# Moving the split weights of a hybrid decoder layer to four different offsets in SBUF

## The chip, the cores and the metric

The kernel runs on one core of a Trainium2 chip. The metric is the device time of one execution in microseconds (us). Before the change it is 892.13 us, the median of three runs (890.99 to 892.81).

## The reference

One decoder layer on x of 512 tokens by 1024 features, in float32: a feed-forward block, a mixing block, and a second feed-forward block, each added to x.

```python
x = x + 0.5 * swiglu(rms_norm(x, g_ffn1), w_ffn1_gate, w_ffn1_up, w_ffn1_down)   # hidden width 2816
h = rms_norm(x, g_mix)
q, k, v, u, mq = split(h @ w_in)          # 512, 128, 128, 512, 256 columns
a = sliding_window_attention(rope(norm(q)), rope(norm(k)), v, sinks)     # 8 heads, window 128
b = conformer_conv(u)                     # GLU, depthwise conv of 31 taps, layer norm, swish
c = memory_cross_attention(norm(mq), mk, mv)   # 4 heads over 256 memory tokens
x = x + concat([a, b, c]) @ w_out
x = x + 0.5 * swiglu(rms_norm(x, g_ffn2), w_ffn2_gate, w_ffn2_up, w_ffn2_down)
```

where `swiglu(h, g, u, d) = (silu(h @ g) * (h @ u)) @ d`.

## The kernel before

**Products in three matmuls.** Features lie in SBUF with the feature index on the 128 partitions and tokens along the free axis. To keep float32 accuracy with one-pass matmuls (type fp32r), each operand is split into a rounded part and the rest, hi and lo, and a product is the sum of three matmuls: hi weights by hi features, hi weights by lo features, lo weights by hi features. `mm3` (L330 to L332) does this for 512 tokens at once, the function `product` (L434 to L436) for 256 tokens. Weights are the operand that is loaded into the array (PEld in the profile), features the one that is moved through it. While one matmul runs, the weights of the next are loaded, so at any time TensorE reads two places of SBUF: the moving tile, and the next weight tile.

**Weights.** The class `Weights` holds a list of loads and of items to be split, in the order in which they are used. `load_to` brings 128x1024 float32 tiles from memory on SyncE's queue (tag `wraw`, four buffers). `split_to` makes hi on ScalarE (L158) and lo on VectorE (L159), three items ahead of use. The hi tiles take turns over four buffers, the lo tiles over four others. In the feed-forward blocks four of the 22 hidden tiles are done directly (gate and up products over eight feature tiles). The other 18 use a fast scheme with seven products of 256 columns instead of eight: `make_sums` adds parts of gate and up weights on VectorE, and the features come as combinations made in `blocks` (tiles `bh` and `bl`). Of the seven products' weights six come from the ring and the seventh from a half tile (`vhi`, `vlo`, 512 columns) with one buffer of its own. Between the fast products stand the down-projections, groups of 512-column matmuls on `hh` and `hl`.

**Mixing.** The order of its steps is written out by hand in the list `ORDER`: projections on 512 columns (`xh`, `xl`), convolution taps on VectorE, scores, softmax, transposes, value products, output products (`yh`, `yl`). `ln_mean` takes the mean over the convolution's channels as a matmul with a constant tile `avg` of 1/256, which `consts` fills on GpSimd at the beginning of the mixing block.

**Where tiles lie.** Each pool is laid out in one piece, a tag after another in the order of their first use, with every tile rounded up to 32 bytes per partition. The ring of weights begins at a multiple of 256: four raw tiles, four hi and four lo tiles of 4096 bytes each, so all of them are at 0 mod 256, and so is the end of this pool. The pool of temporaries begins with a filler of 128 bytes; after it and the small tiles, the pool `act`, which holds the split features (`xh`, `xl`, `hh`, `hl` and part of `yh`, `yl`), begins at 64 mod 256. The pools of the two feed-forward blocks and of mixing follow after it in the same place, one at a time. `ffn` puts a filler of `shift` bytes first (0 in the first block, 64 in the second), and a filler of 192 minus `shift` after the block features. So `bh` and `bl` lie at 64 mod 256 in the first block and at 128 in the second, and the half weight tiles at 0 in both. The distance from a weight tile up to the moving tile, mod 256, is therefore 64 everywhere except for the second block's features, where it is 128. In the memory projection (L630 to L632) the roles are exchanged: weights are moved and features loaded.

Of the kernel before, what the change touches and what calls it, by code (L numbers as in the profile page):

```python
# [28 lines left out]
F32 = mybir.dt.float32  # L29
F32R = mybir.dt.float32r  # L30
# [6 lines left out]
P = 128  # L37
# [10 lines left out]
C_G1, C_GM, C_G2, C_GMEM = 0, 8, 16, 24  # L48
# [26 lines left out]
N_ACT = 20  # L75

SUM_BUFS = 3
MEM_F = 17
B_T3, B_Q1, B_Q2, B_T4, B_21, B_22, B_11 = range(7)


class Weights:
# [5 lines left out]
    def __init__(self, nc, pool, dma_ahead, conv_ahead, bufs):  # L88
        self.nc, self.pool = nc, pool
        self.dma_ahead, self.conv_ahead, self.bufs = dma_ahead, conv_ahead, bufs  # L90
        self.loads, self.items = [], []
        self.raw, self.after, self.split, self.piece = {}, {}, {}, {}
        self.sums = {}
        self.extra = None
        self.by_hand = 2
        self.loaded = self.done = self.at = 0

    def add(self, ap):

# [16 lines left out]
    def make_sums(self, i):  # L116
        nc = self.nc
        g, u = self.raw[i], self.raw[i + 1]
        s12 = self.extra.tile([P, 1024], F32, tag="sum", name=f"s12_{i}", bufs=SUM_BUFS)
        s43 = self.extra.tile([P, 1024], F32, tag="sum", name=f"s43_{i}", bufs=SUM_BUFS)  # L120
        l, r = slice(0, 512), slice(512, 1024)
# [6 lines left out]
    def load_to(self, n):  # L128
        while self.loaded < min(n, len(self.loads)):
            i = self.loaded  # L130
            ap = self.loads[i]
            raw = self.pool.tile([P, 1024], F32, tag="wraw", name=f"wraw{i}", bufs=self.bufs[0])
            self.raw[i] = raw
            if i >= self.by_hand:
                to = raw[:, : int(np.prod(ap.shape[1:]))]
                if len(ap.shape) == 3:
                    to = to.rearrange("p (a b) -> p a b", a=ap.shape[1])
                self.nc.sync.dma_start(to, ap)
            self.loaded += 1

    def split_to(self, n):
        nc = self.nc
        while self.done < min(n, len(self.items)):
            i = self.done
            need, cols, tag, src = self.items[i]
            self.load_to(need + 1)
            if need in self.after:
                self.after.pop(need)()
            pool = self.pool if tag == "w" else self.extra
            width = 1024 if tag == "w" else 512  # L150
            bufs = self.bufs[1:] if tag == "w" else (1, 1)
            hi = pool.tile([P, width], F32R, tag=tag + "hi", name=f"{tag}hi{i}", bufs=bufs[0])
            lo = pool.tile([P, width], F32R, tag=tag + "lo", name=f"{tag}lo{i}", bufs=bufs[1])
            if i < self.by_hand:
                self.piece[i] = (src(), hi, lo)
            else:
                raw = src()
                nc.scalar.copy(hi[:, :cols], raw[:, :cols])  # L158
                nc.vector.tensor_tensor(lo[:, :cols], raw[:, :cols], hi[:, :cols].bitcast(F32), op=ALU.subtract)  # L159
            self.split[i] = (hi, lo)  # L160
            self.done += 1
            if i >= self.by_hand:
                self.load_to(need + 1 + self.dma_ahead)
# [33 lines left out]
def layer(tc, ctx, a):  # L197
    nc = tc.nc
    PE, ACT, DVE, POOL = nc.tensor, nc.scalar, nc.vector, nc.gpsimd

    keep = ctx.enter_context(tc.tile_pool(name="keep", bufs=1))
    wpool = ctx.enter_context(tc.tile_pool(name="wpool", bufs=1))
    tmp = ctx.enter_context(tc.tile_pool(name="tmp", bufs=1))
# [4 lines left out]
    def nm(s):  # L208
        uid[0] += 1
        return f"{s}_{uid[0]}"  # L210
# [14 lines left out]
        return tmp.tile([P, n], F32, tag=f"s{n}", name=nm("s"), bufs=6)  # L225


    W = Weights(nc, wpool, dma_ahead=3, conv_ahead=3, bufs=(4, 4, 4))

    def flat(w):  # L230
        return w.rearrange("p k m -> p (k m)")

    def ffn_weights(n, memory):
        gu = a[f"wgu{n}"]

        def down(r, g):
            lo, hi = ROUNDS[r]
            m = per_load(r)
            return a[f"wd{n}"][g * m : (g + 1) * m, :, lo:hi].rearrange("d p k m -> p d (k m)")

        for f in range(NF):
            pre, mid, post = steps(f)
            for d in pre:
                W.add(down(*d))
            if f < N_DIRECT:
                W.add(flat(gu[f, 0]))
                W.add(flat(gu[f, 1]))
            else:
                W.add_pair(flat(gu[f, 0]), flat(gu[f, 1]), [down(*d) for d in mid])
            for d in post:  # L250
                W.add(down(*d))
            if memory and f == MEM_F:
                for t in range(2):
                    W.add(flat(a["wmk"][t]))
                for c in range(2):
# [17 lines left out]
    par = keep.tile([P, C_N], F32, name="par")  # L273
    ident = keep.tile([P, P], F32, name="ident")
    x = keep.tile([P, KT, T], F32, name="x")
    tmp.tile([P, 32], F32, name="shift")
    act = ctx.enter_context(tc.tile_pool(name="act", bufs=1))
    xh, xl = {}, {}

# [102 lines left out]
    def ffn(pool, norm, first, gain, hooks, next_gain, last, shift):  # L382
# [24 lines left out]
        def blocks(k):  # L407

            raw = pool.tile([P, 4, 256], F32, tag="sum", name=nm("braw"), bufs=SUM_BUFS)
            made = pool.tile([P, 4, 256], F32, tag="sum", name=nm("bmade"), bufs=SUM_BUFS)  # L410
            flat_raw = raw.rearrange("p a b -> p (a b)")
# [136 lines left out]
    norm = Norm()  # L548
# [156 lines left out]
    hooks = {9: [rotary]}  # L705
    hooks[MEM_F - 3] = [lambda: load(0), lambda: load(1)]
    hooks[MEM_F - 2] = [lambda: piece(0), lambda: piece(1), lambda: load(2), lambda: load(3)]
    hooks[MEM_F - 1] = [lambda: piece(2), lambda: piece(3)]
    hooks[MEM_F], hooks[MEM_F + 1] = [sums, p1], [p2]
    with tc.tile_pool(name="fast1", bufs=1) as pool:  # L710
        norm = ffn(pool, norm, STARTS, C_G1, hooks, C_GM, False, 0)

    with tc.tile_pool(name="mix", bufs=1) as mix:
        norm = mixing(tc, nc, a, mix, W, norm, locals())

    with tc.tile_pool(name="fast2", bufs=1) as pool:
        ffn(pool, norm, [[0, 1, 2, 3, 4, 5, 6], [7]], C_G2, {}, None, True, 64)


def mixing(tc, nc, a, mix, W, norm, e):  # L720
    PE, ACT, DVE, POOL = nc.tensor, nc.scalar, nc.vector, nc.gpsimd
    mm_bank, sc_bank, tp_bank, work, small = (e[n] for n in ("mm_bank", "sc_bank", "tp_bank", "work", "small"))
# [12 lines left out]
    vtok = mix.tile([P, NB, P], F32, name="vtok")  # L735
    for i in range(2):
        POOL.memset(pad[:, i, 0:30], 0.0)
    avg = mix.tile([P, P], F32, name="avg")
    maskb = mix.tile([P, 2, T], BF16, name="maskb")
    identb = mix.tile([P, P], BF16, name="identb")  # L740
    nsink = mix.tile([P, 8], F32, name="nsink")
# [1 line left out]
    nc.scalar.dma_start(maskf, a["mask"])  # L743

    def consts():
        POOL.memset(avg, 1.0 / 256.0)
        DVE.tensor_copy(maskb[:, :, 0:256], maskf.unsqueeze(1).to_broadcast([P, 2, 256]))
        DVE.tensor_copy(maskb[:, :, 256:512], maskf.unsqueeze(1).to_broadcast([P, 2, 256]))
        DVE.memset(maskb[:, 0, 0:128], -1e30)
        DVE.tensor_copy(identb, ident)  # L750
        DVE.tensor_scalar(nsink, par[:, C_SINK : C_SINK + 8], -1.0, None, op0=ALU.mult)
# [39 lines left out]
    def pump(n):  # L791
        for _ in range(n):
            next(tap, None)
# [173 lines left out]
    ps_g1 = proj()  # L967
    glu(1, ps_a1, ps_g1)
    consts()

    v = {}
# [64 lines left out]

    def ln_mean():
        pump(TAPS)
        both = work()
        DVE.tensor_tensor(both, conv[:, 0], conv[:, 1], op=ALU.add)  # L1040
        mean = tp_bank()
        PE.matmul(mean, avg, both, start=True, stop=True)
        for i in range(2):
            DVE.tensor_tensor(conv[:, i], conv[:, i], mean, op=ALU.subtract)
# [20 lines left out]
    def ln_swish():  # L1065
# [12 lines left out]
        "sumK": lambda: sums("K", "K"), "facK": key_factor, "normK": key_norm, "turnV": value_turn,  # L1078
        "ropeK": lambda: rope(kT), "c": lambda: pump(1),
        "ln_mean": ln_mean, "ln_square": ln_square, "ln_var": ln_var, "ln_swish": ln_swish,  # L1080
    }
    for t in TILES:
# [121 lines left out]
```

## Time and profile before

| | before |
|---|---|
| runs: median (lowest to highest) | 892.13 us (890.99 to 892.81) |
| the profiled execution's own time | 892.04 us |
| its span, first to last instruction | 890.2 us |
| TensorE matmul busy | 879.2 us (99%) |
| TensorE weight loads busy | 772.4 us (87%) |
| VectorE, ScalarE, GpSimd busy | 713.3, 440.4, 44.4 us |
| mean granted TensorE clock | 0.998 |
| matmuls of `product` on the ring's weights, L434, L435, L436 | 864 each, 281 ns mean duration |

A duration in the profile is that of one matmul from its start to its end, and matmuls overlap: the next begins long before the one before has ended. How fast TensorE goes is read from the starts in the timeline. The profile names tiles without buffer numbers; which buffer an instruction uses follows from its place in the order of the program.

### The profile page before, as it was taken

The numbers are of one execution on the slowest core, as the hardware profiler recorded it, in microseconds if no ns is written. First come the engines' busy times: TensorE is split into PE (matmuls) and PEld (weight loads), VectorE is DVE, ScalarE is ACT, GpSimd is POOL, SyncE is SP. The second block draws the span as 40 slices with busy tenths as digits, with TensorE's granted clock in tenths as the row PEclk, the third lists the DMA queues.
The fourth block names the chain that finished last, engine by engine and source line by source line (L and its number), as shares of the span: only waits on it lengthen the run. The fifth ranks groups of instructions, "written<-read, shape, count | busy, mean of one in ns | idle before, by whom it ended". The sixth has DMA issues, their size and how long they took to land.

```text
span 890.2 us, 14022 instructions
## 1 busy us (share of the span) xinstructions
PE 879.2 (99%) x5525; PEld 772.4 (87%) x5525; DVE 713.3 (80%) x1126; ACT 440.4 (49%) x737; POOL 44.4 (5%) x38
## 2 busy tenths in 40 slices
PE   7999999999999999999999999999999999999998
PEld 4889999999999998887666788889999999999997
DVE  6999988986787976779999775999887767768762
ACT  6454555454474445433838762545554444444440
POOL 6000000000020000300110030000000000000000
PEclk9999999999999999999999999999999999999999
DMA  5522333324335234322010323223232333242312
GB/s 194 166 95 93 98 119 107 119 95 122 104 107 169 83 108 139 94 79 60 24 36 13 108 95 107 84 71 119 95 119 95 96 119 107 66 131 83 114 48 95
DMA packets 34147, 88.46 MB, mean 99 GB/s; under 512 B 3232, under 2 KB 9120, under 8 KB 34080
## 3 DMA queue, kind: packets, MB, share of 16 engines
q1 hardware_dynamic: 32928, 86.00, 30.3%
q10 hardware_dynamic: 1152, 1.57, 0.5%
q8 instruction: 43, 0.70, 0.3%
q14 instruction: 24, 0.20, 0.1%
HBM read 85.45 MB, written 2.10 MB: 98 GB/s over the span
## 4 chain that ended last, share of the span: by engine, by line
PE 94%; DVE 3%; DMA 1%; issue 1%; ACT 0%; SPq 0%; DVEq 0%; ACTq 0%
PE mm L330 15%; PE mm L332 15%; PE mm L331 15%; PE mm L434 11%; PE mm L435 11%; PE mm L436 11%; PE sc L435 2%; PE sc L436 2%; PE sc L434 2%; PE sc L330 1%; PE sc L332 1%; PE sc L331 1%; PE tp L922 1%; PE sc L861 1%; DVE conv L786 1%
## 5 line engine op out<-in xcount | busy, mean ns | idle before, releaser
L434 PE MATMUL mm<-bh,whi 128*128 128x256 f32 x864 | 243.2, 281 | 0.0
L435 PE MATMUL mm<-bl,whi 128*128 128x256 f32 x864 | 243.1, 281 | 0.0
L436 PE MATMUL mm<-bh,wlo 128*128 128x256 f32 x864 | 242.9, 281 | 0.0
L158 ACT CAST whi<-wraw 128x1024 fp32r<-128x1024 f32 (+2 forms) x126 | 125.3, 997 | 129.2 <-PE mm L331 41.5
L159 DVE TENSOR_TENSOR wlo<-wraw,whi 128x1024 fp32r<-128x1024 f32 (+2 forms) x126 | 145.7, 1157 | 34.2 <-ACT whi L158 34.0
L434 PEld LDWEIGHTS mm<-bh,whi 128*128 128x128 f32 x864 | 163.4, 189 | 1.5 <-ACT kept L449 0.2
L435 PEld LDWEIGHTS mm<-bl,whi 128*128 128x128 f32 x864 | 163.2, 189 | 1.1
L436 PEld LDWEIGHTS mm<-bh,wlo 128*128 128x128 f32 x864 | 163.2, 189 | 0.0
L331 PE MATMUL mm<-hl,whi 128*128 128x512 f32 (+1 forms) x356 | 138.4, 390 | 0.0
L332 PE MATMUL mm<-hh,wlo 128*128 128x512 f32 (+1 forms) x356 | 138.1, 389 | 0.0
L330 PE MATMUL mm<-hh,whi 128*128 128x512 f32 (+1 forms) x356 | 137.6, 389 | 0.4 <-ACT whi L158 0.4
L159 DVE TENSOR_TENSOR wlo<-s,whi 128x1024 fp32r<-128x1024 f32 x72 | 87.9, 1222 | 32.2 <-ACT whi L158 30.8
L158 ACT CAST whi<-s 128x1024 fp32r<-128x1024 f32 x72 | 75.6, 1050 | 58.4 <-PE mm L435 40.0
L332 PEld LDWEIGHTS mm<-hh,wlo 128*128 128x128 f32 x356 | 66.9, 188 | 14.2
L332 PE MATMUL mm<-xh,wlo 128*128 128x512 f32 x192 | 77.3, 402 | 1.8 <-DVE wlo L171 1.8
L331 PE MATMUL mm<-xl,whi 128*128 128x512 f32 x192 | 76.7, 399 | 1.6 <-DVE xl L342 1.4
L330 PEld LDWEIGHTS mm<-hh,whi 128*128 128x128 f32 x356 | 66.9, 188 | 12.9 <-ACT whi L158 0.6
L330 PE MATMUL mm<-xh,whi 128*128 128x512 f32 x192 | 77.5, 405 | 0.1
L331 PEld LDWEIGHTS mm<-hl,whi 128*128 128x128 f32 x356 | 67.0, 188 | 12.0
L491 DVE SCALAR_TENSOR_TENSOR x<-mm,x 128x512 f32<-128x512 f32 x88 | 60.0, 686 | 13.6 <-PE mm L332 13.6
L455 ACT ACTIVATE t<-t 128x512 f32<-128x512 f32 x36 | 22.8, 632 | 54.7 <-DVE t L454 54.6
L158 ACT CAST vhi<-wraw 128x512 fp32r<-128x512 f32 x36 | 22.4, 621 | 52.9 <-PE sc L435 43.6
(246 smaller groups left out, 1400.0 us busy)
## 6 DMA issues: line engine op xcount, KB each, us to landing
wraw<-in_wgu SPq DMA_DIRECT2D x86, 512.0 KB, 3.5
wraw<-in_wd SPq DMA_DIRECT2D x32, 512.0 KB, 3.6
wraw<-in_wd SPq DMA_DIRECT2D x16, 384.0 KB, 3.3
wraw<-in_win SPq DMA_DIRECT2D x12, 512.0 KB, 3.5
out<-t SPq DMA_DIRECT2D x7, 256.0 KB, 2.0
x<-in_xT SPq DMA_DIRECT2D x3, 512.0 KB, 5.7
wraw<-in_wout_a SPq DMA_DIRECT2D x6, 256.0 KB, 2.6
t<-in_memT ACTq DMA_DIRECT2D x4, 256.0 KB, 3.4
```

The source lines that it names most:

```text
L158: nc.scalar.copy(hi[:, :cols], raw[:, :cols])
L159: nc.vector.tensor_tensor(lo[:, :cols], raw[:, :cols], hi[:, :cols].bitcast(F32), op=ALU.subtract)
L330: PE.matmul(ps, wh[:, w], hi(k), start=first and i == 0, stop=False)
L331: PE.matmul(ps, wh[:, w], lo(k), start=False, stop=False)
L332: PE.matmul(ps, wl[:, w], hi(k), start=False, stop=last and i == len(ks) - 1)
L434: PE.matmul(ps, wh[:, c], bh[k][:, block], start=one, stop=False, skip_group_check=not first)
L435: PE.matmul(ps, wh[:, c], bl[k][:, block], start=False, stop=False, skip_group_check=not first)
L436: PE.matmul(ps, wl[:, c], bh[k][:, block], start=False, stop=end, skip_group_check=not first)
L455: ACT.activation(g, g, AF.Silu)
L491: DVE.scalar_tensor_tensor(o, ps, 0.5, xd, op0=ALU.mult, op1=ALU.add)
L786: DVE.scalar_tensor_tensor(conv[:, i], pad[:, i, j : j + T], w(i, j), conv[:, i], op0=ALU.mult, op1=ALU.add)
L861: PE.matmul(banks[h][:, i * ML + c.start : i * ML + c.stop], self.q[rows, n * P : (n + 1) * P], self.kt[rows, ks], start=not self.win, sto ...
```

## The change

The single ring of four hi tiles becomes four tags of one hi tile and one lo tile each, used in turn as before. Ahead of the second, third and fourth pair a filler of 32, 128 and 64 bytes is laid, so the pairs begin at 0, 32, 160 and 224 mod 256. The filler ahead of the temporaries grows from 128 to 160 bytes, which with the 224 makes 256: the pools after it keep their offsets mod 256. With the features at 64, the distances from the weights up to the moving tiles are then 64, 32, 160 and 96 bytes. The second block's `shift` becomes 0, which brings its features from 128 to 64 and leaves its half weight tiles at 0. To make room, `avg` is no longer a tile of the mixing pool: `ln_mean` takes one of the five temporary tiles and fills it there.

```diff
+SHIFTS = (0, 32, 128, 64)
...
-        self.loaded = self.done = self.at = 0
+        self.loaded = self.done = self.at = self.turn = 0
...
-            bufs = self.bufs[1:] if tag == "w" else (1, 1)
-            hi = pool.tile([P, width], F32R, tag=tag + "hi", name=f"{tag}hi{i}", bufs=bufs[0])
-            lo = pool.tile([P, width], F32R, tag=tag + "lo", name=f"{tag}lo{i}", bufs=bufs[1])
+            ring = ""
+            if tag == "w":
+                ring = self.turn % len(SHIFTS)
+                if self.turn < len(SHIFTS) and SHIFTS[ring]:
+                    pool.tile([P, SHIFTS[ring] // 4], F32, name=f"shift{ring}")
+                self.turn += 1
+            hi = pool.tile([P, width], F32R, tag=f"{tag}hi{ring}", name=f"{tag}hi{i}", bufs=1)
+            lo = pool.tile([P, width], F32R, tag=f"{tag}lo{ring}", name=f"{tag}lo{i}", bufs=1)
...
-    W = Weights(nc, wpool, dma_ahead=3, conv_ahead=3, bufs=(4, 4, 4))
+    W = Weights(nc, wpool, dma_ahead=3, conv_ahead=3, bufs=4)
...
-    tmp.tile([P, 32], F32, name="shift")
+    tmp.tile([P, 40], F32, name="shift")
...
-        ffn(pool, norm, [[0, 1, 2, 3, 4, 5, 6], [7]], C_G2, {}, None, True, 64)
+        ffn(pool, norm, [[0, 1, 2, 3, 4, 5, 6], [7]], C_G2, {}, None, True, 0)
...
-    avg = mix.tile([P, P], F32, name="avg")
...
     def consts():
-        POOL.memset(avg, 1.0 / 256.0)
...
     def ln_mean():
         pump(TAPS)
-        both = work()
+        both, avg = work(), work()[:, :P]
+        POOL.memset(avg, 1.0 / 256.0)
         DVE.tensor_tensor(both, conv[:, 0], conv[:, 1], op=ALU.add)
         mean = tp_bank()
         PE.matmul(mean, avg, both, start=True, stop=True)
```

More of the change, by code (lines that the diff above doesn't have):

```diff
@@ L131, in load_to @@
             ap = self.loads[i]
-            raw = self.pool.tile([P, 1024], F32, tag="wraw", name=f"wraw{i}", bufs=self.bufs[0])
+            raw = self.pool.tile([P, 1024], F32, tag="wraw", name=f"wraw{i}", bufs=self.bufs)
             self.raw[i] = raw
```

## The prediction

> **What bounds the kernel now.** I read the page first, then the timeline of TensorE, then the windows.
>
> ```profile
> span 890.2 us, 14022 instructions
> PE 879.2 (99%) x5525; PEld 772.4 (87%) x5525; DVE 713.3 (80%) x1126; ACT 440.4 (49%) x737; POOL 44.4 (5%) x38
> PE 94%; DVE 3%; DMA 1%; issue 1%; ACT 0%; SPq 0%; DVEq 0%; ACTq 0%
> L434 PE MATMUL mm<-bh,whi 128*128 128x256 f32 x864 | 243.2, 281 | 0.0
> L331 PE MATMUL mm<-hl,whi 128*128 128x512 f32 (+1 forms) x356 | 138.4, 390 | 0.0
> L332 PE MATMUL mm<-xh,wlo 128*128 128x512 f32 x192 | 77.3, 402 | 1.8 <-DVE wlo L171 1.8
> ```
>
> TensorE holds 94% of the chain that ended last, so a change in the pace of matmuls moves the end. The mean of one (281 ns, 390 ns) is a latency; matmuls overlap. The pace is the distance from one start to the next, and only the timeline shows it. Three stretches with the same code, five products of twelve 256-column matmuls each without a stop; shown are the first start and the next group's first start, 60 matmuls apart:
>
> ```profile
> 182.65 0.28 PE L434 MATMUL mm<-bh,whi 128*128 128x256 f32 x1
> ...
> 189.45 0.39 PE L330 MATMUL mm<-hh,whi 128*128 128x512 f32 x1
> ```
>
> ```profile
> 136.26 0.28 PE L434 MATMUL mm<-bh,whi 128*128 128x256 f32 x1
> ...
> 143.33 0.40 PE L330 MATMUL mm<-hh,whi 128*128 128x512 f32 x1
> ```
>
> ```profile
> 662.03 0.28 PE L434 MATMUL mm<-bh,whi 128*128 128x256 f32 x1
> ...
> 669.23 0.40 PE L330 MATMUL mm<-hh,whi 128*128 128x512 f32 x1
> ```
>
> 6.80, 7.07 and 7.20 us over 60 are **113.3, 117.8 and 120.0 ns** per matmul. The first two are of the first feed-forward block, where moving features lie 64 bytes (mod 256) above the split weights; the third is of the second block, where they lie 128 above. So at 64 there are two paces, and at 128 a third, slower than both. The first block passes from one pace to the other after a stop of a fraction of a us. This one is followed by a last slow group, and then by the fast pace:
>
> ```profile
> 172.62 0.28 PE L436 MATMUL mm<-bh,wlo 128*128 128x256 f32 x1
> 172.91 0.38 PE L434 MATMUL mm<-bh,whi 128*128 128x256 f32 x1
> ```
>
> Before 173 us it is slow throughout and after 177 us mostly fast; I take the midpoint, 115.6 ns, as its mean. The 512-column matmuls all have distance 64; twelve of them in the first and in the second block:
>
> ```profile
> 204.47 0.39 PE L330 MATMUL mm<-hh,whi 128*128 128x512 f32 x1
> ...
> 207.21 0.28 PE L434 MATMUL sc<-bh,vhi 128*128 128x256 f32 x1
> ```
>
> ```profile
> 669.23 0.40 PE L330 MATMUL mm<-hh,whi 128*128 128x512 f32 x1
> ...
> 669.93 0.39 PE L330 MATMUL mm<-hh,whi 128*128 128x512 f32 x1
> ...
> 671.99 0.28 PE L434 MATMUL sc<-bh,vhi 128*128 128x256 f32 x1
> ```
>
> 2.74/12 = 228 ns, 2.76/12 = 230 ns, mean 229.2; the second run's first three, entered from the slow pace, take 0.70 us, 233.3 each.
>
> Is the other work the cause instead? Equal stretches of the two blocks, 500 matmuls each, have the same load on the other engines, and the difference is all in the matmuls:
>
> ```profile
> 75.75:140.03 64.28, 64.28 (x501) 62.26 (x500) 55.60 (x74) 35.20 (x55) 0.00 (x0) 1.00 0.34 107
> 600.79:665.87 65.08, 65.08 (x502) 63.06 (x501) 55.50 (x73) 35.27 (x55) 0.00 (x0) 1.00 0.34 107
> ```
>
> (columns after the length: PE, PEld, DVE, ACT, POOL busy, granted clock, DMA). The clock is 1.00 in both.
>
> **The change, part by part.** No instruction of the feed-forward blocks or projections is added or removed; what changes is where operands lie. The three places given to the first ring positions (32, 128 and 64 bytes) add 224 bytes ahead of the temporary tiles and the grown filler 32 more, 256 together: so every moving tile stays where it was mod 256, and the change does do what its name says. Costs by part:
>
> *1. Second block back from 128 to 64.* Counts: 864 per line and three lines are 2592 matmuls on the ring's weights; the 512-wide halves (v tiles) have their own row:
>
> ```profile
> L434 PE MATMUL sc<-bh,vhi 128*128 128x256 f32 x144 | 40.4, 281 | 0.0
> ```
>
> 432 more. Half of each is the second block's: 1296 + 216 = 1512. After the change 216 (v tiles stay at offset 0) and a quarter of 1296, 324, run at distance 64: 540 × (120.0 − 115.6) = **−2.4 us**; at its slow pace throughout −1.2, at its fast one −3.6.
>
> *2. 256-column matmuls on ring positions 1 to 3, distances 32, 160, 96.* No row has these distances. 96 lies between 64 (113.3 to 117.8) and 128 (120.0). 160 lies between 128 and 192, and 192 has a row: in the memory projection the weights move and the features (64 above) are the loaded side:
>
> ```profile
> 286.09 0.28 PE L630 MATMUL mm<-whi,mh 128*128 128x256 f32 x1
> ...
> 286.77 0.28 PE L630 MATMUL mm<-whi,mh 128*128 128x256 f32 x1
> ```
>
> Six steps in 0.68 us, 113.3 ns. 32 has a neighbour on one side only (64); for 0 there is no row. Bounds 113.3 and 120.0 for all three, and I take the middle, 116.7: each of 96 and 160 has one good and one bad neighbour, and 32 is nearest to a good one with the other unseen. 972 matmuls per block. Second block: 972 × (120.0 − 116.7) = **−3.2 us**; first block: 972 × (116.7 − 115.6) = **+1.1 us**. By the bounds −6.5 to 0 and −2.2 to +4.3.
>
> *3. 512-column matmuls.* 3 × 356 and 3 × 192 by the first fence, less 24 halves at the end, 1620; the smaller groups of the attention outputs are not counted. Three quarters, 1215, get a new distance. Bounds: twice 113.3 = 226.7 below, 233.3 above, against 229.2: −3.0 to +5.0 us. The middle, 230.0, would be +1.0; I take **0**, since 228 and 230 are what whole groups show and 233.3 only three steps at an entry, and an entry from the slow pace occurs less often afterwards.
>
> *4. Rings.* Four tags with one buffer each instead of one tag with four: the tiles already took turns, so each waits for the same earlier release; nothing is issued more or later. Cover for faster matmuls: the weights must be split in time.
>
> ```profile
> 177.00:252.00 75.00, 74.56 (x529) 69.16 (x527) 58.41 (x78) 36.65 (x58) 2.19 (x2) 1.00 0.34 108
> 617.00:760.00 143.00, 143.00 (x1001) 134.14 (x1000) 111.07 (x144) 68.96 (x105) 0.00 (x0) 1.00 0.32 102
> ```
>
> The fast stretch of the first block ran with VectorE 78% busy and PE busy 74.56 of 75.00 us. The second block's VectorE is also at 78%; if its matmuls reach 113.3, that becomes 82%, which is still covered. VectorE's splits do not feel the distance of their operands (source 64 above in the first line's block, raw tiles at 0 in the second line):
>
> ```profile
> L159 DVE TENSOR_TENSOR wlo<-s,whi 128x1024 fp32r<-128x1024 f32 x24 | 29.3, 1221 | 9.1 <-ACT whi L158 8.4 <-PE mm L436 0.7
> L159 DVE TENSOR_TENSOR wlo<-wraw,whi 128x1024 fp32r<-128x1024 f32 x20 | 24.4, 1222 | 5.7 <-ACT whi L158 5.7
> ```
>
> *5. The averaging tile* is now filled by GpSimd inside the layer norm's mean, in a temporary tile from the ring of five.
>
> ```profile
> 467.91 1.29 POOL L833 TENSOR_TENSOR t<-t,sinb 128x512 f32<-128x512 f32 x1 [9.90 <-DVE t L832]
> 524.14 1.31 POOL L359 TENSOR_TENSOR sqsum<-sqsum,t 128x512 f32<-128x512 f32 x1 [54.95 <-ACT t L355]
> 347.08 0.20 POOL L746 MEMSET avg<- 128x128 f32 x1
> 500.29 1.02 PE L1042 MATMUL tp<-t,avg 128*128 128x512 f32 x2
> L835 DVE TENSOR_TENSOR q<-t,t x4: 677/684/694, 444.3 to 475.1; 128x512 f32<-128x512 f32 x4
> ```
>
> The fill takes 0.20 us. GpSimd is idle from 469.2 to 524.1, the rotations that used the ring before end at 475.8, and TensorE needs the tile at 500.3: 24 us of cover, cost 0. Without cover it would be 0.2 us plus the wait for a slot on TensorE, with the score and output matmuls queued behind it; the ring's later users (squares at 502, the spread at 508) each get a slot that is free by then.
>
> Sum: −2.4 − 3.2 + 1.1 + 0 + 0 = −4.5 us against the profiled execution's 892.04 us (span 890.2 and 1.8 around it; the median 892.13 is 0.1 above): **887.5 us**.
>
> The Trainium skill, TensorE: Matmul & The Clock Gate (Part 2, step ① on LDWEIGHTS), says that TensorE has two independent SBUF read ports and that loading the next weights takes no read bandwidth from the running matmul. By that rule the layout is free and the time would stay at 892.0. The three paces of one instruction form speak against it here, which is why that case gets a small chance below. The same page's back-to-back gap (N/2.4 + 2.5 ns) gives an estimate of 109 and 216 ns; no group in this trace ran at it.
>
> **The rivals.**
>
> *A: every new distance holds the fast pace,* because a change of distance at each new weight tile breaks the slow lock. Both blocks at 113.3: 1512 × 6.7 = −10.1 and 1512 × (115.6 − 113.3) = −3.5: **878.4 us**. For it: the fast pace survives whole stretches with down-projections between (177 to 252 us), and 192 is fast too. Against: 128 never is.
>
> *B: slower.* All three new distances are odd multiples of 32, while every distance seen is a multiple of 64. If reads go in 64-byte pieces, a weight slice of 512 bytes that begins 32 off touches nine pieces instead of eight and shares one with the moving stream wherever that stands. Price: the step between fast and 128, so 120.0 for 972 in each block (first +4.3, second 0), 233.3 for the 512-column ones (+5.0), and only the 540 at distance 64 gain (−2.4): **898.9 us**. It decides from where the new distances' 256-column pace passes 119.0 ns: there 972 × (2 × 119.0 − 115.6 − 120.0) eats the 2.4 us. For it: 120 is a distance's price in the trace; against: only 128 shows it, and 32 is farther from that than 64 is.
>
> *C: distance isn't the cause;* the second block's pace is a lock it fell into, as the first block fell into its two, and it stays there: **892.0 us**. For it: the paces persist and change only with stops. Against: the 120.0 is never seen in the first block, nor 113.3 in the second.
>
> **How the numbers follow.** Forecast 0.47 (its own range 883 to 891, from part 1's and a third of part 2's bounds), A 0.20, B 0.20, C 0.13. A measurement of this kernel tells about 0.2% (1.8 us) from no change. Faster: A, and 0.45 of the forecast's 0.47, 0.65. Same: C and a little of the forecast, 0.14. Slower: B and the rest, 0.21. All bounds at their good ends give 892.0 − 10.1 − 3.5 − 3.0 = 875.4, at their bad ones 892.0 − 1.2 + 4.3 + 5.0 = 900.1. The range 877 to 897 leaves out the far half of B and the last of A.
>
> **What would show it.** In the second block's 256-column stretches, starts 113 to 118 ns apart on weights of ring position 0 and on v tiles (part 1); paces that change with the weight tile, every 12 or 24 matmuls (part 2); groups of twelve 512-column matmuls still near 2.75 us (part 3); no wait of TensorE on weight splits in the blocks (4), and none on GpSimd at the layer norm (5). Wrong it would be if paces were the same on all ring positions, if one new distance passed 120 ns, or if the 512-column groups moved by more than 2%.

## The result and the profile after

The changed kernel takes 897.46 us (median of three, 897.18 to 898.28) against 892.13: a ratio of 1.0064, 95% interval 1.0041 to 1.0086. It is slower by 5.3 us, where 4.5 us less was forecast. From the page of the changed kernel (its lines are shifted: `mm3` is now L336 to L338, `product` L440 to L442):

```profile
span 895.6 us, 14020 instructions
PE 884.4 (99%) x5525; PEld 772.2 (86%) x5525; DVE 713.6 (80%) x1126; ACT 440.1 (49%) x737; POOL 44.8 (5%) x38
PE 94%; DVE 3%; DMA 1%; ACT 1%; issue 0%; SPq 0%
L440 PE MATMUL mm<-bh,whi 128*128 128x256 f32 x864 | 242.4, 281 | 0.0
```

The page looks the same but for 5.2 us more of busy TensorE; the chain that ended last has nearly the same shares, and the mean duration of a matmul is still 281 ns. Two stretches without a stop, one behind the other, show where the time is. The first is the three down-projection groups ahead of the second block's fast scheme, 72 matmuls of 512 columns. The second is the fast scheme's first hidden tile and the first five of the seven products of its second, 144 matmuls of 256 columns, twelve of them on a half tile. Timeline of TensorE of the kernel before, the first start of each and of what follows (columns: start, duration, engine, line, operation):

```profile
584.31 0.39 PE L330 MATMUL mm<-hh,whi 128*128 128x512 f32 x1
...
600.79 0.28 PE L434 MATMUL mm<-bh,whi 128*128 128x256 f32 x1
...
617.87 0.39 PE L330 MATMUL mm<-hh,whi 128*128 128x512 f32 x1
```

The same of the changed kernel, with the start of the first block's fast scheme ahead:

```profile
76.56 0.28 PE L440 MATMUL mm<-bh,whi 128*128 128x256 f32 x1
...
590.80 0.39 PE L336 MATMUL mm<-hh,whi 128*128 128x512 f32 x1
...
607.53 0.28 PE L440 MATMUL mm<-bh,whi 128*128 128x256 f32 x1
...
624.52 0.39 PE L336 MATMUL mm<-hh,whi 128*128 128x512 f32 x1
```

The 512-column matmuls went from 16.48/72 = 228.9 ns to 16.73/72 = 232.4, the 256-column ones from 17.08/144 = 118.6 to 16.99/144 = 118.0. At the first fast product of the first block the changed kernel is 0.8 us behind (75.75 before), at that of the second 6.7, at the end 5.4: the rest of the second block wins back 1.3. Adding up the time from each start to the next over both traces, stops included, the 512-column matmuls on split weights cost 5.8 us more, the 256-column products 2.4 more in the first block and 2.6 less in the second. Everything else is 0.2 shorter, and together this is the 5.4.

Within the second block the pace changes with the ring position. Four neighbouring groups of the changed kernel: 24 matmuls at distance 160, 24 at 96, 12 at 64, then twelve 512-column ones at 32:

```profile
668.05 0.28 PE L440 MATMUL mm<-bh,whi 128*128 128x256 f32 x1
...
670.87 0.28 PE L440 MATMUL mm<-bh,whi 128*128 128x256 f32 x1
...
673.75 0.28 PE L440 MATMUL mm<-bh,whi 128*128 128x256 f32 x1
...
675.16 0.40 PE L336 MATMUL mm<-hh,whi 128*128 128x512 f32 x1
...
677.95 0.28 PE L440 MATMUL sc<-bh,vhi 128*128 128x256 f32 x1
```

117.5, 120.0, 117.5 and 232.5 ns. No stretch of the fast scheme stays at 113.3 any more. The averaging tile costs nothing: GpSimd fills it right after its last rotation, long before the layer norm, and goes idle again.

```profile
474.27 0.21 POOL L1044 MEMSET t<- 128x128 f32 x1
529.79 1.30 POOL L365 TENSOR_TENSOR sqsum<-sqsum,t 128x512 f32<-128x512 f32 x1 [55.30 <-ACT t L361]
```

### The profile page after: what moved, and what is told of

It is laid out like the page before. It is cut to its first block, busy times and chain, and to the rows that moved or that the text cites. A ratio compares the mean times of both kernels' runs of the same rounds, so it can differ in the third digit from the quotient of the medians.

```text
span 895.6 us, 14020 instructions
## 1 busy us (share of the span) xinstructions
PE 884.4 (99%) x5525; PEld 772.2 (86%) x5525; DVE 713.6 (80%) x1126; ACT 440.1 (49%) x737; POOL 44.8 (5%) x38
## 4 chain that ended last, share of the span: by engine, by line
PE 94%; DVE 3%; DMA 1%; ACT 1%; issue 0%; SPq 0%
PE mm L336 15%; PE mm L338 15%; PE mm L337 15%; PE mm L440 11%; PE mm L441 11%; PE mm L442 11%; PE sc L442 2%; PE sc L440 2%; PE sc L441 2%; PE sc L337 1%; PE sc L338 1%; PE sc L336 1%; PE tp L926 1%; PE sc L865 1%; DVE conv L790 1%; DMA x<-in_xT 1%
## 5 line engine op out<-in xcount | busy, mean ns | idle before, releaser
L440 PE MATMUL mm<-bh,whi 128*128 128x256 f32 x864 | 242.4, 281 | 0.0
L442 PE MATMUL mm<-bh,wlo 128*128 128x256 f32 x864 | 241.8, 280 | 0.0
L440 PEld LDWEIGHTS mm<-bh,whi 128*128 128x128 f32 x864 | 162.4, 188 | 1.3
L442 PEld LDWEIGHTS mm<-bh,wlo 128*128 128x128 f32 x864 | 162.4, 188 | 0.0
L338 PE MATMUL mm<-hh,wlo 128*128 128x512 f32 (+1 forms) x356 | 139.0, 392 | 0.0
L336 PE MATMUL mm<-hh,whi 128*128 128x512 f32 (+1 forms) x356 | 138.7, 392 | 0.0
L338 PEld LDWEIGHTS mm<-hh,wlo 128*128 128x128 f32 x356 | 66.8, 188 | 15.6
L338 PE MATMUL mm<-xh,wlo 128*128 128x512 f32 x192 | 77.3, 403 | 2.3 <-DVE wlo L177 2.3
L336 PE MATMUL mm<-xh,whi 128*128 128x512 f32 x192 | 77.5, 406 | 0.9 <-ACT whi L176 0.9
L336 PEld LDWEIGHTS mm<-hh,whi 128*128 128x128 f32 x356 | 66.8, 188 | 13.1
```

The source lines that it names most:

```text
L336: PE.matmul(ps, wh[:, w], hi(k), start=first and i == 0, stop=False)
L338: PE.matmul(ps, wl[:, w], hi(k), start=False, stop=last and i == len(ks) - 1)
L440: PE.matmul(ps, wh[:, c], bh[k][:, block], start=one, stop=False, skip_group_check=not first)
L442: PE.matmul(ps, wl[:, c], bh[k][:, block], start=False, stop=end, skip_group_check=not first)
```

## The experiments

All of them start from the changed kernel and move only where tiles lie, except for the last four, which also add a matmul. Ratios are against the kernel before, run on the same chip. Paces named "over the trace" are means over all starts of a class in the profiled execution, stops left out; those of 256 columns are of the ring's weights. The 1815 of the expectations is a count of 512-column steps; the kernel has 1908 such matmuls on split weights.

**1. Each part alone.** The second block's features at 64, all weights at 0:

```diff
-SHIFTS = (0, 32, 128, 64)
+SHIFTS = (0, 0, 0, 0)
-    tmp.tile([P, 40], F32, name="shift")
+    tmp.tile([P, 32], F32, name="shift")
```

> All weight tiles at offset 0 as before the change, second block's features at 64: part 1 of the prediction alone, for all 1512 matmuls of 256 columns of the second block. Theory 'distance' (the prediction's): second block between 113.3 and 117.8 ns, in the mean the first block's 115.7 instead of 119.8, 1512 x 4.1 = 6.2 us gained, 886 us; 512-column matmuls unchanged at 229. Rival C (distance isn't the cause): second block stays at 120, 892 us.

Measured: 889.78 us, ratio 0.9964 (0.9949 to 0.9979). The 144 matmuls of the second block's fast scheme that took 17.08 us before:

```profile
602.73 0.28 PE L440 MATMUL mm<-bh,whi 128*128 128x256 f32 x1
...
619.69 0.40 PE L336 MATMUL mm<-hh,whi 128*128 128x512 f32 x1
```

16.96/144 = 117.8 ns, and the whole second block runs at 117.8, not 120, so its offset had been the cause and rival C falls; but it stays at the slow pace of distance 64 throughout, and the first block too has less of the fast one (116.9 over the trace, 115.8 before). Moved for all of the second block, the features gain 2 to 3 us and not the 6 expected. Twelve executions of this one program lie between 885.99 and 890.79.

The other part alone, four offsets with the second block's features kept at 128:

```diff
-        ffn(pool, norm, [[0, 1, 2, 3, 4, 5, 6], [7]], C_G2, {}, None, True, 0)
+        ffn(pool, norm, [[0, 1, 2, 3, 4, 5, 6], [7]], C_G2, {}, None, True, 64)
```

> The four offsets of the changed kernel, but the second block's features at 128, so that its 256-column distances are 128, 96, 224 and 160. Theory 'the new distances cost the 512-column matmuls' (233 instead of 229 on three ring positions): the 512-column matmuls stay at 233, and the second block's 256-column ones go from 118.2 back to about 119 to 120: 899 to 900 us. If instead the second block's return to 64 caused the loss, this one is at 892 or below.

Measured: 898.76 us, 1.0074 (1.0056 to 1.0092). The four offsets make the loss; the move of the second block's features gains about 1 us on top (1.1 by the traces; the two intervals overlap).

**2. One distance at a time, without alternation.** All four ring positions at one offset, with the filler of the temporaries such that everything else stays in place, here for offset 32:

```diff
-SHIFTS = (0, 32, 128, 64)
+SHIFTS = (32, 0, 0, 0)
-    tmp.tile([P, 40], F32, name="shift")
+    tmp.tile([P, 24], F32, name="shift")
```

> All weight tiles of the ring at one offset, 32, so that all distances are 32 (half tiles: 64). Theory 1 (a weight slice that begins 32 bytes off a 64-byte piece costs one more step): 512-column matmuls at about 233 with no alternation at all, 256-column ones near 117.6, time 892 + 1815 x 3.6 ns + about 0 = 898 us. Theory 2 (alternation: each change of distance throws the reads out of their lock, a single distance settles): 512-column at 226 to 229 and 256-column at 113 to 115, 882 to 888 us.

> All weight tiles of the ring at one offset, 160, so that all distances are 160 (half tiles: 64). Theory 1 (32 bytes off a piece): 512-column matmuls at about 233.7, 256-column near 117.9, 892 + 1815 x 4.3 ns + 0.4 = 900 us. Theory 2 (alternation): 512-column at 226 to 229, 256-column at 113 to 116, 882 to 889 us.

Measured: distance 32 takes 896.61 us, 1.0049 (1.0032 to 1.0066); distance 160 takes 900.29 us, 1.0092 (1.0074 to 1.0111). Both are near what theory 1 expected, and alternation is not needed for the loss. The two stretches at distance 32:

```profile
590.40 0.39 PE L336 MATMUL mm<-hh,whi 128*128 128x512 f32 x1
...
607.20 0.28 PE L440 MATMUL mm<-bh,whi 128*128 128x256 f32 x1
...
623.96 0.39 PE L336 MATMUL mm<-hh,whi 128*128 128x512 f32 x1
```

16.80/72 = 233.3 and 16.76/144 = 116.4 ns.

**3. The weights' own place, or the distance?** Two kernels separate them: both sides moved by 32 (distance 64, both off a multiple of 64), and only the moving tiles put at 32 (distance 32, weights at 0).

```diff
+SHIFTS = (32, 0, 0, 0)                          # both moved
+    tmp.tile([P, 32], F32, name="shift")
...
+SHIFTS = (0, 0, 0, 0)                           # moving tiles at 32
+    tmp.tile([P, 24], F32, name="shift")
```

> All weight tiles at offset 32 and all moving tiles at 96: the distance is 64 as before, but both sides begin 32 bytes off a multiple of 64. Theory 1a (it is the weights' own place: a slice at an odd multiple of 32 covers nine 64-byte pieces): 512-column matmuls at 233, 256-column near 117.5, 897 us. Theory 1b (it is the distance alone): 512-column at 229.4, 256-column between 113.3 and 117.8, 886 to 890 us, as with all offsets at 0 and 64.

> All weight tiles at offset 0, all moving tiles at 32: distance 32, as in the run with the weights at 32, but with the weights on multiples of 64. Theory 1a (the weights' own place): 512-column matmuls at about 229, 256-column between 113 and 118, 886 to 890 us. Theory 1b (the distance alone): 512-column 233.2, 256-column 117.0, 896.6 us, the same as with the weights moved.

Measured: both moved, 886.57 us, 0.9939 (0.9910 to 0.9969), with 229.4 ns for 512 columns over the trace of an execution of 891.44; only the moving tiles moved, 896.61 us, 1.0059 (1.0035 to 1.0082), with 233.2 and 117.1 ns over the trace, as with the weights moved (233.2 and 117.0). The first of the two stretches, with both moved:

```profile
586.89 0.39 PE L336 MATMUL mm<-hh,whi 128*128 128x512 f32 x1
...
603.37 0.28 PE L440 MATMUL mm<-bh,whi 128*128 128x256 f32 x1
```

16.48/72 = 228.9 ns, exactly as with the weights at 0 and the features at 64. For these two distances, 32 and 64, the distance decides and not the weights' own place; the theory of nine 64-byte pieces falls.

**4. The other distances.** The same edit with other offsets.

> All weight tiles of the ring at offset 64: distance 0 to all moving tiles (half tiles 64). No row has this distance. Theories 1a and 1b (an even multiple of 32 costs the 512-column matmuls nothing): 512-column at 229, time 886 to 892 us by the 256-column pace of 113 to 120. Rival (two reads in the same 256-byte place collide at every step): 512-column above 233 and 256-column above 120, 900 us or more.

> All weight tiles of the ring at offset 128: distance 192 (half tiles 64). The memory projection, with weights and features exchanged, ran at 113.3 at this distance. Theories 1a and 1b: 512-column at 229 or below, 256-column 113.3 if the row of the memory projection carries over, 892 - 3.2 - 8.4 = 880 us; 885 to 890 if it has the same two paces as 64.

Measured: distance 0, 894.67 us, 1.0032 (1.0019 to 1.0045); distance 192, 891.20 us, 0.9991 (0.9979 to 1.0003). The two stretches at distance 0, then at 192:

```profile
588.65 0.39 PE L336 MATMUL mm<-hh,whi 128*128 128x512 f32 x1
...
604.98 0.28 PE L440 MATMUL mm<-bh,whi 128*128 128x256 f32 x1
...
622.17 0.40 PE L336 MATMUL mm<-hh,whi 128*128 128x512 f32 x1
```

```profile
588.07 0.39 PE L336 MATMUL mm<-hh,whi 128*128 128x512 f32 x1
...
604.87 0.28 PE L440 MATMUL mm<-bh,whi 128*128 128x256 f32 x1
...
621.19 0.39 PE L336 MATMUL mm<-hh,whi 128*128 128x512 f32 x1
```

Distance 0 has the fastest 512-column matmuls (16.33/72 = 226.8 ns) and slow 256-column ones (17.19/144 = 119.4); 192 has 233.3 and 113.3. Neither came as expected: at 0 the time lies between theory and rival, and at 192 the 512-column matmuls eat what the 256-column ones gain. Multiples of 64 are not free, and the two widths rank the distances differently. The remaining ones:

> All weight tiles of the ring at offset 192: distance 128 (half tiles 64). Distance theory: 256-column at 119.8 in both blocks, as the second block before the change: +1296 x 4 = 5.2 us; 512-column unknown, 228 to 234. 895 to 905 us.

> All weight tiles of the ring at offset 224: distance 96 (half tiles 64). Distance theory, by the changed kernel's rows of this distance: 256-column 119.8, 512-column 233.3; 892 + 1296 x 4 ns + 1815 x 3.9 ns - 0.5 = 904 us. If a single distance settles better than the mix does: 895 or less.

> All weight tiles of the ring at offset 96: distance 224 (half tiles 64). Distance theory, by the run with the second block at 128 that has this distance for 256 columns: 118.3, and 512-column between 228 (distance 0) and 233 (192), 231: 892 + 1296 x 2.5 - 1296 x 1.5 + 1815 x 1.6 = 896 us.

Measured: 899.67 us, 1.0091 (1.0068 to 1.0113); 903.76 us, 1.0135 (1.0109 to 1.0162); 899.80 us, 1.0090 (1.0068 to 1.0112). Distances 128 and 96 took the times expected, 224 more than its 896, as its 512-column matmuls went to 233.1 and not 231. Over the traces, in ns from start to start (half tiles are at 64 in all rows):

| distance | 512 columns | 256 columns, first and second block | ratio of times |
|---|---|---|---|
| 0 | 228.1 | 119.8, 119.8 | 1.0032 |
| 32 | 233.2 | 117.1, 116.9 | 1.0049 |
| 64 | 229.4 | 116.9, 117.8 | 0.9964 |
| 96 | 233.2 | 120.0, 120.0 | 1.0135 |
| 128 | 232.7 | 118.7, 118.7 | 1.0091 |
| 160 | 234.1 | 118.0, 118.0 | 1.0092 |
| 192 | 233.2 | 114.7, 115.2 | 0.9991 |
| 224 | 233.1 | 118.4, 118.4 | 1.0090 |

The changed kernel is this table's mean: its 512-column matmuls, at 64, 32, 160 and 96 in turn, have 232.6 over its trace. Of its three new distances none was good for them. One row shows that the 256-column pace is not set by the distance alone: at 128 it is 118.7 here, where 119.8 was expected because the second block of the kernel before had that over its trace at the same distance. There the half tiles were at 128 too, and the 512-column groups in between at 64.

**5. Each width at its own distance.** Moving tiles of 512 columns at 0, block features at 192, all weights at 0:

```diff
-    tmp.tile([P, 32], F32, name="shift")
+    tmp.tile([P, 16], F32, name="shift")
-                pool.tile([P, (192 - shift) // 4], F32, name=nm("shift"))
+                pool.tile([P, 16], F32, name=nm("shift"))
-        norm = ffn(pool, norm, STARTS, C_G1, hooks, C_GM, False, 0)
+        norm = ffn(pool, norm, STARTS, C_G1, hooks, C_GM, False, 192)
-        ffn(pool, norm, [[0, 1, 2, 3, 4, 5, 6], [7]], C_G2, {}, None, True, 0)
+        ffn(pool, norm, [[0, 1, 2, 3, 4, 5, 6], [7]], C_G2, {}, None, True, 192)
```

(against the version with all weights at 0 of experiment 1; for block features at 64, below, the filler after them is 48 floats, and the blocks' `shift` is 64.)

> Weights all at offset 0; the features of the 512-column matmuls at 0 (distance 0), those of the 256-column products at 192 (distance 192), each at the best distance found for its width. Theory 'each width has its own table of distances, and the two add': 512-column 228.05 instead of 229.4 (1815 x 1.4 = 2.5 us), 256-column 114.9 in both blocks (1512 x 0.9 + 1512 x 4.9 = 8.8 us): 881 us. Rival: the pace of 192 came with the 512-column matmuls of the same run, in between; then the 256-column ones go to 118 and the time is 887 or more.

Measured: 887.88 us, 0.9955 (0.9939 to 0.9971), faster than both kernels. The 512-column part came as expected, the rival came for the other:

```profile
585.25 0.39 PE L336 MATMUL mm<-hh,whi 128*128 128x512 f32 x1
...
601.57 0.28 PE L440 MATMUL mm<-bh,whi 128*128 128x256 f32 x1
...
618.53 0.39 PE L336 MATMUL mm<-hh,whi 128*128 128x512 f32 x1
```

16.32/72 = 226.7 and 16.96/144 = 117.8 ns: at 192 too there are two paces, and here it is the slow one.

> As the version with 512-column features at 0 and block features at 192, but block features at 64. Distance theory with two paces for both 64 and 192: 512-column 227, 256-column 117.8 (slow pace) as at 192, 887 to 888 us; if 64 falls into its fast pace here, 113.3 in both blocks, 1512 x 2 x 4.4 = 13 us less, 875 us.

Measured: 890.36 us, 0.9989 (0.9979 to 0.9999). Again the slow pace in both blocks, but not the 887 to 888 us expected with it: the 512-column matmuls lose a little at their entries (228.4 over the trace, 227.2 with 192).

**6. What chooses between the two paces.** One additional short matmul, result unused, ahead of two of the eighteen hidden tiles of the fast scheme in each block, of 32, 64 or 128 columns:

```diff
             s12, s45, g, u = kept(), kept(), work(), work()
+            if f in (N_DIRECT, 20):
+                PE.matmul(tp_bank()[:, :128], bh[0][:, B_11, :P], bh[0][:, B_11, :128], start=True, stop=True)
```

> The version with distances 0 and 192, and one additional matmul of 32 columns (result unused) on TensorE ahead of the first fast product, and of the one of hidden tile 20, in both blocks. Theory 'phase' (the pace of the 256-column matmuls is a state handed on from group to group; the products enter it in one of several phases): one of the lengths 32, 64, 128 throws the products into the fast pace, 113.3 from there on, up to 13 us less, 875 to 882 us; those that don't stay at 117.8 and 888 us. Rival 'place' (the slow pace belongs to this set of addresses): all three lengths stay at 117.8, 888 us.

> The same with an additional matmul of 64 columns. Theory 'phase': 875 to 882 us for at least one of the three lengths, 888 for the others. Rival 'place': 888 us for all.

> The same with an additional matmul of 128 columns. Theory 'phase': 875 to 882 us for at least one of the three lengths, 888 for the others. Rival 'place': 888 us for all.

Measured: 886.91 us, 0.9945 (0.9928 to 0.9963); 888.41 us, 0.9963 (0.9951 to 0.9976); 886.77 us, 0.9943 (0.9924 to 0.9961). With 128 columns, first block:

```profile
75.52 0.22 PE L450 MATMUL tp<-bh 128*128 128x128 f32 x1
75.58 0.33 PE L440 MATMUL mm<-bh,whi 128*128 128x256 f32 x1
...
91.98 0.39 PE L336 MATMUL mm<-hh,whi 128*128 128x512 f32 x1
```

16.40/144 = 113.9 ns, from the same instructions at the same addresses that took 117.8 without it (16.96 us, from 75.09 to 92.05). 32 columns do the same (16.42 us), 64 do not (17.04). The times are not the 875 to 882 expected, because the fast pace ends at the next 512-column group. So the pace depends on what runs just ahead of a group, and not on the addresses alone; that this is a phase, as the theory has it, is argued and not shown. The last run puts the short matmul ahead of every hidden tile that follows a 512-column group. The last two products of a tile, which come behind the down-projection in its middle, get none:

```diff
+            if wide[0]:
+                PE.matmul(tp_bank()[:, :128], bh[0][:, B_11, :P], bh[0][:, B_11, :128], start=True, stop=True)
...
+            wide[0] = False      # ahead of the last down-projections of a hidden tile
...
+                wide[0] = True   # in each down-projection
```

> Distances 0 and 192, and the additional matmul of 128 columns (about 0.11 us) ahead of every fast product that follows a 512-column group. Theory 'phase': every such entry then takes the fast pace, so the stretches of 60 matmuls take 6.85 instead of 7.07 us and those of 228 about 26.0 instead of 26.8, less 0.11 each: some 2 us better than with it at two places only, 884 to 885 us. If the entry depends on more than the last group: 888 to 890 us, the cost of the additional matmuls alone.

Measured: **885.34 us**, 0.9919 (0.9905 to 0.9933), close to the 884 to 885 expected and the lowest median of all; the version with both sides moved by 32 (0.9910 to 0.9969) is not told apart from it.

```profile
599.94 0.33 PE L440 MATMUL mm<-bh,whi 128*128 128x256 f32 x1
...
616.33 0.39 PE L336 MATMUL mm<-hh,whi 128*128 128x512 f32 x1
```

The products take 16.39/144 = 113.8 ns, and over the trace 114.4 and 114.1 on the ring's weights in the two blocks, against 117.3 and 117.8 without the short matmul. Where a tile's last two products follow a down-projection, they stay at 117.8.

## Why the prediction was wrong

*What bounds the kernel, and that distance sets the pace:* right. The losses and gains are in the starts of matmuls; distance 32, whether made from the weights' side or from the features' side, gives the same paces (experiment 3). By the Trainium skill (TensorE: Matmul & The Clock Gate, Part 2, step ①) the two reads have ports of their own, and loading the next weights takes no read bandwidth from the running matmul. By that rule the distance would cost nothing; the runs do not agree, with 226.7 ns (distance 0) to 233.3 (32, 192) for 512 columns in a stretch without stops.

*Part 3, the 512-column matmuls:* this step failed, and it is more than half of the miss. I took 0, because whole groups had shown only 228 and 230 ns. But all those groups had distance 64, which is one of the two good ones; the three new distances run at 233.2 to 234.1. The upper bound, 233.3, was about the right value, and with the groups that the count had left out it comes to 5.8 us. The mark set for being wrong here, 2%, was too coarse: 229.5 to 232.6 ns over the traces is 1.4%. Groups that share one layout say nothing on another. The rest of the miss is in parts 1 and 2: 4.5 us of gain were forecast for the 256-column matmuls, and 0.2 came.

*Part 2, the 256-column matmuls at the new distances:* the middle of the bounds, 116.7 ns, was low. In the changed kernel 96 has about 119.8, 160 about 117.9 and 32 about 117.6. The interpolation between neighbours misled: 96 is as bad as 128 was, or worse.

*Part 1, the second block's features:* right in sign, too large. I gave distance 64 the midpoint of its two paces, 115.6. In the changed kernel it runs at about 117.5, and the first block's 113.3 is gone as well, so that block loses 2.4 us where 1.1 was allowed. Which pace occurs depends on what runs just ahead (experiment 6), and the changed groups ahead of the products probably alter that; the midpoint was no estimate of it.

*Parts 4 and 5:* right. After the first 25 us no matmul of the changed kernel waits for split weights, and the averaging tile cost nothing.

*The rivals.* A falls: a single distance keeps its pace without alternation, and in the mix the fast pace was lost. B came nearest (898.9 against 897.46), with its price right for the 512-column matmuls (233.3 ns). That the sum came so near is in part luck: it had 120.0 for all new distances of the 256-column matmuls, which only 96 has. Its mechanism is refuted: both sides moved by 32 cost nothing, and 192, a multiple of 64, costs the 512-column matmuls as much as 32. C falls by the second block's step from 120 to 117.8 when it was moved alone.

Not settled: why these distances and widths rank as they do, and whether it is the two reads that meet. No run looks inside the reads.

## What to carry to other kernels

Where weights are loaded while features are moved, as here, treat the distance of the two in SBUF mod 256 as a parameter: in this kernel it was worth up to 6 ns per matmul. Each matmul width needs its own measurement: one run per distance, read from start to start in a stretch without stops. Don't infer a distance from its neighbours, nor one width from another; and the mix of four distances was only as good as the mean of the four. Put each kind of moving tile at its best one instead, and measure the combination, since the gains of the two widths did not add up here (experiment 5).

## What the runs showed of the hardware that was not expected

Two widths of the same instruction want different distances: at 0 the 512-column matmuls have their best pace (226.7 ns in a steady stretch) and the 256-column ones a poor one (119.8), at 192 it is the other way round (233.3 and 113.3). At 64 and 192 the 256-column matmuls have two steady paces, 113.3 and 117.8. In the layout of experiment 5, at 192, a matmul of 32 or 128 columns ahead of them moves them from the slow to the fast one at the same addresses, while one of 64 columns does not. The choice probably differs from execution to execution of one program, too: the version with both sides moved by 32 had ten between 881.41 and 892.10 us, where four at distance 160 lay between 899.82 and 900.81. Only one of the ten was profiled, so their paces are not shown.
